# Stick-breaking half of the output projection begun between the pieces of the latent attention's preparation

## The chip, the cores and the metric

The kernel runs on one core of one Trainium2 chip. The metric is the device time of one execution in microseconds (us), given as the median of several runs. Names of engines in the profile: PE is TensorE's matmul queue, PEld its weight loads, DVE is VectorE, ACT ScalarE, POOL GpSimd, SP SyncE.

## The reference

Two transformer blocks act on 512 tokens of width 1024. The first is a hybrid of pooling and forgetting attention. The change lies in the second, which runs two attentions of 8 heads side by side, joins them, and then runs a feed-forward block over product keys. Cut to what matters:

```python
h = rms_norm(x, attn_norm)
sb_q, sb_k, sb_v, cq, ckv, k_pe = split(h @ w_in)
sb = stick_breaking_attention(sb_q, sb_k, sb_v)            # (512, 512)
q = rms_norm(cq, cq_norm) @ w_uq                           # 8 heads of 96
k_nope, v = split(rms_norm(ckv, ckv_norm) @ w_ukv)         # 8 heads of 64 + 64
k = concat(k_nope, k_pe)                                   # 8 heads of 96
q, k = rope_tail(rms_norm(q, q_norm)), rope_tail(rms_norm(k, k_norm))
mla = chunk_causal_softmax_attention(q, k, v)              # (512, 512)
mixed = concat(rms_norm(sb, sb_out_norm), rms_norm(mla, mla_out_norm))
x = x + mixed @ w_o                                        # (512, 1024) @ (1024, 1024)
x = x + peer_ffn(rms_norm(x, ffn_norm), ...)
```

The two norms before `w_o` are separate, so the half of the product that takes `sb` can be computed before `mla` is known.

## The kernel before

Tokens are kept in four tiles of 128 (`TT`). Weights come as a stream of units: a DMA on SP's queue into `wraw`, then a split into a high and a low part (`whi` by ACT, `wlo` by DVE or POOL, L129 and L130), each with two buffers. `unit(k, n)` takes the next unit of the stream and splits it if that hasn't been done; `ahead()` splits one unit more. Products use both parts: `mm3` issues three matmuls (L150 to L152) for each block of 128 rows.

In the second block two generators run against each other. The main one is `both`: first `sb_attention` (24 steps, three `yield`s in each, two or three heads' worth of scores, log, scan, exponential, transposes and values), then `ml_attention` (22 steps of scores, maximum, exponential, transposes, values). The other one, `fill`, holds everything that is done beside them: `heads_qk` (queries and keys of the stick-breaking heads), `prep` (the latent attention's preparation: cq and ckv with their norms, `uq_half`, `q_norm`, `uk_half`, `k_norm`, and `heads_T`, the transposes of the finished heads) and `after_prep`. For each `yield` of the main one, `fill` is advanced 0.65 steps during the stick-breaking attention (`RATE1`) and one step after it. Where the main one needs something of `fill` (scores of a query tile whose keys aren't there), it advances `fill` until it has come.

`after_prep` starts when `prep` is through and `sb_attention` has ended. It asks for the two rows of gains for the norms (`rows2`, in the buffer "ck", which `prep` uses for the latent keys), puts the norm of the stick-breaking half into the list `todo` (`o_norm`, three pieces for each token tile: `n0` sum of squares and reciprocal root, `n1` scaling, `n2` four transposes into the bank "mi" and the split into `mxs_hi` and `mxs_lo`), and takes one piece of `todo` at every second step. From its step 20 (`WP0`) on, every third step issues one tile of `wo_part`: two column halves of four token tiles each, 12 matmuls with 512 columns into "mi", which DVE adds to `xres`. The latent half's norms come into `todo` as its query tiles are done; its part of the projection comes after both attentions, with the final norm (`last2`).

A scheduler puts the instructions into the engines' queues. It goes by the order of the program as a priority and takes an instruction earlier where its inputs and buffers are there by its reckoning. Each engine then works through its own queue in order.

Of the kernel before, what the change touches and what calls it, by code (L numbers as in the profile page):

```python
# [11 lines left out]
F32R = mybir.dt.float32r  # L12
# [9 lines left out]
T = 512  # L22
TT = 4
# [14 lines left out]
ROWS = {}  # L38
# [22 lines left out]
def hybrid_mla_peer_kernel(ctx: ExitStack, tc: tile.TileContext, x, meta, gains, rows, bforget, wf, w1v, w1u, poolw,  # L61
                           wup, wout, pos, w2v, w2u, wcq, wckv, wuq, wukv, wo, wpq, skT, uT, peer_u, peer_v, out, stop=None):
    nc = tc.nc
    V, S, G, PE = nc.vector, nc.scalar, nc.gpsimd, nc.tensor
# [29 lines left out]
    def tB(shape, name, dt=F32, tag=None):  # L94
        return pB.tile(shape, dt, name=name, tag=tag, bufs=2 if tag == "sc" else 1)
# [18 lines left out]
    def load_next():  # L114
        i = st["load"]
        if i < len(stream):
            n = stream[i].shape[1]
            r = strm.tile([128, 2048], F32, name="wraw", tag="wraw")
            nc.sync.dma_start(r[:, :n], stream[i])
            raws[i] = (r, n)  # L120
            st["load"] += 1

    def split_next():
        i = st["split"]
        if i < len(stream):
            r, n = raws.pop(i)
            hi = strm.tile([128, 2048], F32R, name="whi", tag="whi")
            lo = strm.tile([128, 2048], F32R, name="wlo", tag="wlo")
            S.activation(hi[:, :n], r[:, :n], AF.Copy)  # L129
            lo_eng["e"].tensor_tensor(lo[:, :n], r[:, :n], hi[:, :n].bitcast(F32), op=OP.subtract)  # L130
            splits[i] = (hi, lo)
            st["split"] += 1

    def unit(k, n):
        i = st["use"]
        st["use"] += 1
        while st["split"] <= i:
            split_next()
            load_next()
        hi, lo = splits.pop(i)  # L140
        pat = "p (k n) -> p k n"
        return (hi[:, :k * n].rearrange(pat, k=k), lo[:, :k * n].rearrange(pat, k=k))

    def ahead():
        if st["split"] <= st["use"]:
            split_next()
            load_next()
# [10 lines left out]
    def row_of(dst, name, eng=None):  # L158
        o, w = ROWS[name]
        (eng or nc.scalar).dma_start(dst, rows[:, o:o + w].to_broadcast([dst.shape[0], w]))  # L160

    def rstd_from_ss(ss, n, p=128, cols=1):
        t = small.tile([128, 8], F32, name="rs_t", tag="rs_t")
        r = small.tile([128, 8], F32, name="rs_r", tag="rs_r")
        V.tensor_scalar(t[:p, :cols], ss, 1.0 / n, EPS, op0=OP.mult, op1=OP.add)
        G.tensor_tensor(r[:p, :cols], t[:p, :cols], mhalf[:p, :cols], op=OP.pow)
        return r[:p, :cols]
# [574 lines left out]
    with ExitStack() as c2:  # L742
        p2 = c2.enter_context(tc.tile_pool(name="p2", bufs=1))

        def t2(shape, name, dt=F32, tag=None, bufs=None):
            return p2.tile(shape, dt, name=name, tag=tag or name, bufs=bufs)
# [17 lines left out]
        row_of(mrow, "qk")  # L764
        crow = t2([128, 640], "crow")
        row_of(crow, "ckv")
        posf = t2([128, TT], "posf")
        V.tensor_copy(posf, posi)
        invf = t2([128, 16], "invf")
# [59 lines left out]
        sso, mv = so_[:, 0], so_[:, 1]  # L829
# [6 lines left out]
        def rope_ops(dst, src, tt, heads):  # L836

            c = cs[:, 0, tt, :].unsqueeze(1).to_broadcast([128, heads, 16])
            s = cs[:, 1, tt, :].unsqueeze(1).to_broadcast([128, heads, 16])
            ra = t2([128, 8, 16], "ra", bufs=2)[:, :heads]  # L840
            rb = t2([128, 8, 16], "rb", bufs=2)[:, :heads]
            a, b = src[:, :, 0:16], src[:, :, 16:32]
            G.tensor_tensor(ra, a, c, op=OP.mult)
            G.tensor_tensor(rb, b, s, op=OP.mult)
            ra2 = t2([128, 8, 16], "ra", bufs=2)[:, :heads]
            rb2 = t2([128, 8, 16], "rb", bufs=2)[:, :heads]
            G.tensor_tensor(ra2, a, s, op=OP.mult)
            G.tensor_tensor(rb2, b, c, op=OP.mult)
            G.tensor_tensor(dst[:, :, 0:16], ra, rb, op=OP.subtract)
            G.tensor_tensor(dst[:, :, 16:32], ra2, rb2, op=OP.add)  # L850

        def prep():
# [56 lines left out]
            def q_norm(tt):  # L909
                q = cn["qn", tt]  # L910
                ss8 = small.tile([128, 8], F32, name="ss8", tag="sum1")
                V.tensor_reduce(ss8, cn.pop(("ss", tt)), axis=AX.X, op=OP.add)
                r = rstd_from_ss(ss8, 96, cols=8)
                yield
                V.tensor_tensor(q, q, r.unsqueeze(2).to_broadcast([128, 8, 96]), op=OP.mult)
                rope_ops(q[:, :, 64:96], q[:, :, 64:96], tt, 8)
                yield
# [31 lines left out]
            def heads_T(which, tt, hg):  # L949
                if which not in mqk:  # L950
                    mqk[which] = tA([96, 8, T], "m" + which, tag="qk" if which == "qn" else "vz")
                src, dst = cn[which, tt], mqk[which]
                b = mm_bank()
                for hh in range(4):
                    PE.transpose(b[:96, tok(hh)], src[:, 4 * hg + hh, :], ident)
                bv = b[:96, :].rearrange("p (h t) -> p h t", h=4)
                (S.copy if hg else V.tensor_copy)(dst[:, 4 * hg:4 * hg + 4, tok(tt)], bv)
                yield
# [15 lines left out]
            for tt in range(1, TT):  # L974
# [9 lines left out]
                yield from nq  # L984
                yield from uq_half(us, tt, 1)
            u = unit(2, 1024)
            nq = q_norm(3)
            next(nq)
            yield from heads_T("qn", 1, 0)
# [13 lines left out]
            for tt in (1, 2, 3):  # L1003
                nk = k_norm(tt)
                next(nk)
                yield from heads_T("kn", tt - 1, 0)
                if tt < 3:
                    yield from uk_half(u, tt + 1, 0)
                yield from nk
                yield from heads_T("kn", tt - 1, 1)  # L1010
                mready.add(tt - 1)
                if tt < 3:
                    yield from uk_half(u, tt + 1, 1)
                if tt == 2:
                    ahead()
            yield from heads_T("kn", 3, 0)
            yield from heads_T("kn", 3, 1)
# [86 lines left out]
        todo = []  # L1104
        mixed = {}
        keep = {}
# [3 lines left out]
        def o_norm(src, key, half, tt):  # L1110
            def n0():
                keep[key] = col_of(p2, src, T)

            def n1():
                V.scalar_tensor_tensor(src, src, keep.pop(key), mixed["row"][:, half * 512:(half + 1) * 512],
                                       op0=OP.mult, op1=OP.mult)

            def n2():
                b = tr_tile(src, range(4), "mi", 1)
                dst = mixed[key[0]]  # L1120
                split_evac(dst[0][:, :, tok(tt)], dst[1][:, :, tok(tt)], b.rearrange("p (k t) -> p k t", k=4))

            return [n0, n1, n2]
# [56 lines left out]
        def wo_part():  # L1180

            for n in range(2):
                u = unit(4, 512)
                for tt in range(TT):
                    o = bank("mi", 1)
                    mm_group(o, lambda k: sel_of(mixed["s"], k, tok(tt)), u, 4)
                    if tt == 0:
                        ahead()
                    d = xres[:, tt, n * 512:(n + 1) * 512]
                    V.tensor_tensor(d, d, o, op=OP.add)  # L1190
                    yield

        def after_prep():

            rows2 = t2([128, 2, D], "rows2", tag="ck")
            mixed["row"], mixed["ffn"] = rows2[:, 0, :], rows2[:, 1, :]
            row_of(mixed["row"], "mix")
            row_of(mixed["ffn"], "ffn")
            mixed["s"] = (tB([128, 4, T], "mxs_hi", F32R, tag="sc"), tB([128, 4, T], "mxs_lo", F32R, tag="sc"))
            mixed["m"] = (tB([128, 4, T], "mxm_hi", F32R, tag="ut"), t2([128, 4, T], "mxm_lo", F32R, tag="cq"))  # L1200
            todo[0:0] = [f for qt in range(TT) for f in o_norm(sso[:, qt, :], ("s", qt), 0, qt)]
            wp = wo_part()
            cnt = 0
            while True:
                cnt += 1
                if todo and cnt % 2 == 0:
                    todo.pop(0)()
                if cnt >= WP0 and cnt % WPS == 0:
                    next(wp, None)
                if mixed.get("end"):  # L1210
                    for _ in wp:
                        pass
                    return
                yield

        def fill2():
            yield from heads_qk()
            yield from prep()
            while "sb_done" not in mixed:
                yield  # L1220
            yield from after_prep()

        def both(fill):
            yield from sb_attention(fill)
# [623 lines left out]
```

## Time and profile before

| | us |
|---|---|
| median of 3 runs | 2022.26 |
| lowest and highest | 2018.98, 2022.57 |
| the profiled execution | 2021.11 |
| its span in the trace | 2019.2 |
| TensorE busy in it | 1950.6 (97%) |
| DVE, ACT, POOL busy | 1372.6, 770.9, 582.2 |

Times in the rows below are microseconds from the start of the span. The stick-breaking attention ends at about 620, the latent attention at about 720, the projection and the final norm at about 760; the feed-forward block takes the rest. In the timeline a row gives the start, the duration, the engine, the line, the operation, output<-inputs, the count and, in brackets, how long the engine had stood idle before it and what released it. Ends of matmuls are modelled and overlap, so the time of one in a row of many is the distance of their starts.

### The profile page before, as it was taken

What the parts mean: (1) busy time and instruction counts of PE and PEld (TensorE: products, weight loads), DVE (VectorE), ACT (ScalarE), POOL (GpSimd) and SP (SyncE); (2) the same over time, 40 slices, a digit from 0 to 9 for tenths busy, and PEclk for the clock granted to TensorE, in tenths of its full rate; (3) what the DMA queues carried; (4) which work ended last, traced back from release to release, by engine and by line L of the source; (5) the groups of instructions that cost most, each with busy time, mean ns of one, the idle gap of its engine ahead of it and who ended that gap; (6) DMA issues with size and microseconds to landing.
All of it is one profiled execution on the core that took longest, in us unless ns stands there. A gap on an engine that the chain in (4) does not pass through costs nothing.

```text
span 2019.2 us, 26981 instructions
## 1 busy us (share of the span) xinstructions
PE 1950.6 (97%) x10297; PEld 1671.7 (83%) x10297; DVE 1372.6 (68%) x2571; ACT 770.9 (38%) x1228; POOL 582.2 (29%) x479
## 2 busy tenths in 40 slices
PE   7999999999998989999888999999999999999999
PEld 5777688877886779889888888888888888888887
DVE  4233423564476668999898677777777777787785
ACT  4223323254575442223555333333333333333332
POOL 1001100200147015655100143333333434343441
PEclk9999999999998999999999999999999999999999
DMA  4211122422111133213788888988888888888885
GB/s 150 97 63 42 42 84 88 142 92 73 36 54 63 42 136 105 94 43 105 225 251 243 288 305 320 317 310 312 286 316 286 315 318 314 307 321 296 308 297 191
DMA packets 138129, 387.63 MB, mean 192 GB/s; under 512 B 10624, under 2 KB 59904, under 8 KB 129808
## 3 DMA queue, kind: packets, MB, share of 16 engines
q1 hardware_dynamic: 48576, 216.65, 29.9%
q0 software_dynamic: 36864, 134.23, 19.5%
q10 hardware_dynamic: 52560, 35.03, 5.9%
q8 instruction: 80, 1.31, 0.3%
q14 instruction: 49, 0.40, 0.1%
HBM read 357.04 MB, written 28.84 MB: 191 GB/s over the span
## 4 chain that ended last, share of the span: by engine, by line
PE 73%; DMA 11%; DVE 7%; issue 4%; POOL 3%; ACT 2%; SPq 0%; DVEq 0%; POOLq 0%; ACTq 0%
PE mm L150 12%; PE mm L152 12%; PE mm L151 12%; DMA gat<-in_peer_v,idx 8%; PE s L151 3%; PE s L150 3%; PE s L152 3%; PE pt L151 3%; PE pt L152 3%; PE pt L150 3%; DMA gat<-in_peer_u,idx 2%; PE mi L150 1%; PE mi L152 1%; PE mi L151 1%; PE av L1044 1%
## 5 line engine op out<-in xcount | busy, mean ns | idle before, releaser
L1616 POOL DMA_INDIRECT gat<-in_peer_u,idx x128 | 172.0, 1344 | 413.0 <-DVE pre L1630 201.5
L1616 POOL DMA_INDIRECT gat<-in_peer_v,idx x128 | 166.4, 1300 | 265.0 <-DVE pre L1630 146.6
L1634 DVE SCALAR_TENSOR_TENSOR acc<-gat,pre,acc 128x1024 f32<-128x1024 f32 x128 | 164.1, 1282 | 77.1 <-DMA gat<-in_peer_v,idx 76.4
L152 PE MATMUL mm<-h_hi,ulo 128*128 128x384 f32 x568 | 192.2, 338 | 6.8 <-DVE ulo L1390 5.3
L1630 DVE CUSTOM_DVE_ANT_0 gat<-gat,xt 128x1024 f32<-128x1024 f32 x128 | 155.7, 1221 | 56.0 <-DMA gat<-in_peer_u,idx 55.5
L150 PE MATMUL mm<-h_hi,uhi 128*128 128x384 f32 x568 | 193.0, 340 | 0.0
L151 PE MATMUL mm<-h_lo,uhi 128*128 128x384 f32 x568 | 191.6, 337 | 0.0
L130 DVE TENSOR_TENSOR wlo<-wraw,whi 128x2048 fp32r<-128x2048 f32 (+1 forms) x42 | 96.0, 2285 | 136.4 <-ACT whi L129 136.3
L1389 ACT ACTIVATE vhi<-xt 128x1024 fp32r<-128x1024 f32 x94 | 99.5, 1059 | 215.2 <-PE mi L152 109.0
L152 PE MATMUL mm<-h_hi,h_lo 128*128 128x384 f32 x456 | 153.3, 336 | 4.5 <-POOL h_lo L1390 2.5
L150 PE MATMUL mm<-h_hi 128*128 128x384 f32 x456 | 153.9, 337 | 0.0
L151 PE MATMUL mm<-h_lo,h_hi 128*128 128x384 f32 x456 | 152.7, 335 | 0.0
L1390 DVE TENSOR_TENSOR vlo<-xt,vhi 128x1024 fp32r<-128x1024 f32 x94 | 114.7, 1221 | 53.6 <-ACT vhi L1389 53.4
L129 ACT ACTIVATE whi<-wraw 128x2048 fp32r<-128x2048 f32 (+2 forms) x53 | 97.5, 1840 | 110.7 <-PE mm L151 58.9
L152 PEld LDWEIGHTS mm<-h_hi,ulo 128*128 128x128 f32 x568 | 107.5, 189 | 8.7 <-DVE ulo L1390 6.9
L150 PEld LDWEIGHTS mm<-h_hi,uhi 128*128 128x128 f32 x568 | 107.6, 189 | 1.9
L151 PEld LDWEIGHTS mm<-h_lo,uhi 128*128 128x128 f32 x568 | 107.6, 189 | 1.9
L150 PE MATMUL mm<-hT_hi,whi 128*128 128x512 f32 x256 | 105.1, 410 | 1.3 <-DVE fz L417 1.0
L150 PE MATMUL s<-vhi,w_hi 128*128 128x512 f32 x256 | 100.3, 392 | 5.0 <-ACT w_hi L1710 5.0
L152 PE MATMUL mm<-hT_hi,wlo 128*128 128x512 f32 x256 | 102.2, 399 | 0.0
L151 PE MATMUL mm<-hT_lo,whi 128*128 128x512 f32 x256 | 102.1, 399 | 0.0
L151 PE MATMUL s<-vlo,w_hi 128*128 128x512 f32 x256 | 100.7, 393 | 0.0
(578 smaller groups left out, 5062.0 us busy)
## 6 DMA issues: line engine op xcount, KB each, us to landing
xt<-in_uT SPq DMA_DIRECT2D x98, 512.0 KB, 5.2
xt<-in_peer_v SPq DMA_DIRECT2D x94, 512.0 KB, 5.9
Gd<-stage ACTq DMA_DIRECT2D x24, 1024.0 KB, 5.3
gate<-Gd SPq DMA_DIRECT2D x16, 1536.0 KB, 10.0
raw<-in_peer_v SPq DMA_DIRECT2D x34, 512.0 KB, 5.4
wraw<-in_w1u SPq DMA_DIRECT2D x16, 1024.0 KB, 4.8
raw<-in_uT SPq DMA_DIRECT2D x30, 512.0 KB, 5.5
wraw<-in_wpq SPq DMA_DIRECT2D x8, 1024.0 KB, 4.8
```

The lines of the kernel that those rows point to most:

```text
L129: S.activation(hi[:, :n], r[:, :n], AF.Copy)
L130: lo_eng["e"].tensor_tensor(lo[:, :n], r[:, :n], hi[:, :n].bitcast(F32), op=OP.subtract)
L150: PE.matmul(o, L[0], R[0], start=start, stop=False)
L151: PE.matmul(o, L[0], R[1], start=False, stop=False)
L152: PE.matmul(o, L[1], R[0], start=False, stop=stop)
L1044: PE.matmul(av[:, col(h, qt):col(h, qt) + 64], pts[i][:, c + j * 128:c + (j + 1) * 128], src[:, j, h * 64:(h + 1) * 64], start=(j == 0), s ...
L1389: S.activation(hi, src, AF.Copy)
L1390: eng.tensor_tensor(lo, src, hi.bitcast(F32), op=OP.subtract)
L1616: G.indirect_dma_start(out=t, out_offset=None, in_=peer_u if kind == "u" else peer_v, in_offset=bass.IndirectOffsetOnAxis(ap=idx[:, s:s + ...
L1630: V.tensor_tensor_reduce(t, t, xt0, 1.0, 0.0, op0=OP.mult, op1=OP.add, accum_out=pre[:, s:s + 1])
L1634: V.scalar_tensor_tensor(acc, t, pre[:, s:s + 1], acc, op0=OP.mult, op1=OP.add)
```

## The change

- A tile `mrow0` of 128 x 512 is added; it gets the gains of the stick-breaking half's norm by a DMA on ACT's queue, at the start of the second block, and `n1` of that half reads it in place of `rows2`.
- `fill2` runs `prep` piece by piece. Once the stick-breaking attention has ended, each of its steps runs one piece of `after_prep` ahead of one piece of `prep`.
- `after_prep` first takes the 12 norm pieces of the stick-breaking half (in an order that staggers the token tiles) and then, when the unit of `w_ukv` has been taken from the stream, the four tiles of the first column half of `wo_part`. When `prep` is through it goes on as before with the rows, what is left of the norm pieces, and the second column half from step 20 on.
- Two `ahead()` calls get conditions, and one is added behind `prep`, so that the splits follow the new order of the units.

```diff
--- before.py
+++ after.py
@@ -764,6 +764,9 @@
         row_of(mrow, "qk")
         crow = t2([128, 640], "crow")
         row_of(crow, "ckv")
+        mrow0 = t2([128, 512], "mrow0")
+        o_ = ROWS["mix"][0]
+        nc.scalar.dma_start(mrow0, rows[:, o_:o_ + 512].to_broadcast([128, 512]))
         posf = t2([128, TT], "posf")
         V.tensor_copy(posf, posi)
         invf = t2([128, 16], "invf")
@@ -984,6 +987,7 @@
                 yield from nq
                 yield from uq_half(us, tt, 1)
             u = unit(2, 1024)
+            mixed["ukv"] = True
             nq = q_norm(3)
             next(nq)
             yield from heads_T("qn", 1, 0)
@@ -1011,7 +1015,7 @@
                 mready.add(tt - 1)
                 if tt < 3:
                     yield from uk_half(u, tt + 1, 1)
-                if tt == 2:
+                if tt == 2 and "wo" not in mixed:
                     ahead()
             yield from heads_T("kn", 3, 0)
             yield from heads_T("kn", 3, 1)
@@ -1112,7 +1116,7 @@
                 keep[key] = col_of(p2, src, T)
 
             def n1():
-                V.scalar_tensor_tensor(src, src, keep.pop(key), mixed["row"][:, half * 512:(half + 1) * 512],
+                V.scalar_tensor_tensor(src, src, keep.pop(key), mixed["row"][:, 512:1024] if half else mrow0,
                                        op0=OP.mult, op1=OP.mult)
 
             def n2():
@@ -1184,7 +1188,8 @@
                 for tt in range(TT):
                     o = bank("mi", 1)
                     mm_group(o, lambda k: sel_of(mixed["s"], k, tok(tt)), u, 4)
-                    if tt == 0:
+                    mixed["wo"] = mixed.get("wo", 0) + 1
+                    if tt == 0 and "prep_done" in mixed:
                         ahead()
                     d = xres[:, tt, n * 512:(n + 1) * 512]
                     V.tensor_tensor(d, d, o, op=OP.add)
@@ -1192,14 +1197,24 @@
 
         def after_prep():
 
+            mixed["s"] = (tB([128, 4, T], "mxs_hi", F32R, tag="sc"), tB([128, 4, T], "mxs_lo", F32R, tag="sc"))
+            parts = [o_norm(sso[:, qt, :], ("s", qt), 0, qt) for qt in range(TT)]
+            mine = [parts[i][k] for w in range(6) for i, k in ((w, 0), (w - 1, 1), (w - 2, 2)) if 0 <= i < TT]
+            wp = wo_part()
+            while "prep_done" not in mixed:
+                if mine:
+                    mine.pop(0)()
+                elif "ukv" in mixed and mixed.get("wo", 0) < TT:
+                    next(wp)
+                yield
             rows2 = t2([128, 2, D], "rows2", tag="ck")
             mixed["row"], mixed["ffn"] = rows2[:, 0, :], rows2[:, 1, :]
             row_of(mixed["row"], "mix")
             row_of(mixed["ffn"], "ffn")
-            mixed["s"] = (tB([128, 4, T], "mxs_hi", F32R, tag="sc"), tB([128, 4, T], "mxs_lo", F32R, tag="sc"))
             mixed["m"] = (tB([128, 4, T], "mxm_hi", F32R, tag="ut"), t2([128, 4, T], "mxm_lo", F32R, tag="cq"))
-            todo[0:0] = [f for qt in range(TT) for f in o_norm(sso[:, qt, :], ("s", qt), 0, qt)]
-            wp = wo_part()
+            todo[0:0] = mine
+            if mixed.get("wo", 0) > 0:
+                ahead()
             cnt = 0
             while True:
                 cnt += 1
@@ -1215,10 +1230,18 @@
 
         def fill2():
             yield from heads_qk()
-            yield from prep()
+            p, a = prep(), None
+            while "prep_done" not in mixed:
+                if next(p, p) is p:
+                    mixed["prep_done"] = True
+                    break
+                yield
+                if "sb_done" in mixed:
+                    a = a or after_prep()
+                    next(a)
             while "sb_done" not in mixed:
                 yield
-            yield from after_prep()
+            yield from a or after_prep()
 
         def both(fill):
             yield from sb_attention(fill)
```

## Rows read from the trace of the kernel before

**Rows 1.** The page, part 1: busy us, share, instructions by engine.

```profile
PE 1950.6 (97%) x10297; PEld 1671.7 (83%) x10297; DVE 1372.6 (68%) x2571; ACT 770.9 (38%) x1228; POOL 582.2 (29%) x479
```

**Rows 2.** Stretches: length, busy us by engine, granted clock, DMA share, GB/s.

```profile
620.00:630.00 10.00, 7.00 (x28) 5.39 (x29) 7.13 (x11) 5.24 (x15) 8.82 (x10) 0.83 0.53 197
630.00:640.00 10.00, 8.39 (x49) 6.37 (x48) 4.50 (x13) 3.42 (x10) 7.69 (x8) 1.00 0.03 11
...
650.00:660.00 10.00, 9.14 (x73) 7.89 (x72) 7.58 (x17) 7.16 (x20) 4.51 (x6) 1.00 0.14 53
660.00:710.00 50.00, 50.00 (x286) 38.88 (x285) 28.07 (x46) 19.53 (x48) 1.59 (x3) 1.00 0.12 43
```

**Rows 3.** Timeline of TensorE, gaps: start, us, instruction [idle <-releaser].

```profile
620.80 1.05 PE L955 MATMUL mm<-ident,qn 128*96 128x128 f32 x8 [0.81 <-ACT mqn L957]
622.56 0.78 PE L150 MATMUL mm<-whi,ck 128*128 128x512 f32 x1 [0.70 <-ACT mqn L957]
628.66 0.64 PE L955 MATMUL mm<-ident,qn 128*96 128x128 f32 x4 [1.50 <-POOL qn L850]
631.96 0.50 PE L150 MATMUL mm<-whi,ck 128*128 128x512 f32 x1 [0.83 <-ACT mqn L957]
634.85 0.50 PE L150 MATMUL mm<-whi,ck 128*128 128x512 f32 x1 [0.78 <-DVE mkn L957]
646.67 0.64 PE L955 MATMUL mm<-ident,qn 128*96 128x128 f32 x4 [0.62 <-POOL qn L945]
652.44 1.08 PE L955 MATMUL mm<-ident,qn 128*96 128x128 f32 x8 [0.85 <-POOL qn L945]
```

**Rows 4.** First norm's instructions (ns min/median/max, first, last start); DMA (KB, us to landing).

```profile
L171 ACT ACTIVATE junkb<-so x4: 629/630/632, 621.3 to 623.9; 128x512 bf16<-128x512 f32 x4
646.02 0.33 ACTq L160 DMA_DIRECT2D rows<-in_rows  x1
rows<-in_rows ACTq DMA_DIRECT2D x2, 512.0 KB, 3.5
652.35 2.23 POOL L166 TENSOR_TENSOR rs_r<-rs_t,mhalf 128x1 f32<-128x1 f32 x4
L1115 DVE SCALAR_TENSOR_TENSOR so<-so,rs_r,rows x4: 740/740/752, 652.9 to 666.3; 128x512 f32<-128x512 f32 x4
L156 DVE TENSOR_TENSOR mxs_lo<-mi,mxs_hi x4: 680/690/691, 659.6 to 673.7; 128x512 fp32r<-128x512 f32 x4
```

**Rows 5.** Tiles of the projection: their group, two timeline rows.

```profile
L150 PE MATMUL mi<-whi,mxs_hi x32: 392/399/800, 666.2 to 708.7; 128*128 128x512 f32 x32
675.76 0.39 PE L152 MATMUL mi<-whi,mxs_lo 128*128 128x512 f32 x1
677.86 0.40 PE L152 MATMUL mi<-whi,mxs_lo 128*128 128x512 f32 x1
```

**Rows 6.** Timeline of POOL and DVE, 620 to 651.

```profile
623.48 3.04 POOL L843 TENSOR_TENSOR ra<-qn,cs 128x128 f32<-128x128 f32 x1 [1.07 <-DVE qn L915]
623.92 2.28 DVE L130 TENSOR_TENSOR wlo<-wraw,whi 128x2048 fp32r<-128x2048 f32 x1
626.48 0.47 POOL L844 TENSOR_TENSOR rb<-qn,cs 128x128 f32<-128x128 f32 x1
630.45 1.65 POOL L166 TENSOR_TENSOR rs_r<-rs_t,mhalf 128x8 f32<-128x8 f32 x1 [0.46 <-DVE rs_t L165]
649.55 1.64 POOL L166 TENSOR_TENSOR rs_r<-rs_t,mhalf 128x8 f32<-128x8 f32 x1 [2.25 <-DVE rs_t L165]
```

**Rows 7.** Timeline of TensorE at the end of the latent attention.

```profile
711.38 1.00 PE L1044 MATMUL av<-so,pts 128*128 128x64 f32 x8
713.19 0.61 PE L1037 MATMUL pt<-ident,sbf 128*128 128x128 f32 x4
713.64 1.00 PE L1044 MATMUL av<-so,pts 128*128 128x64 f32 x8
```

## Prediction

> **What bounds the kernel now.** I read the page first [rows 1]: TensorE is busy 97% of the span, so a change of the order alone can only win time where TensorE stands idle or runs at its lower clock. Then the table of stretches around the place that the change touches [rows 2]: before 660 us TensorE idles (busy 7.00 of 10 us in 620 to 630, 8.39 in the next, 9.14 in 650 to 660); from 660 to 710 it shows no idle time at all. Its granted clock is 0.83 of full in 620 to 630, a part of that stretch being spent at 1.2 GHz and the rest at 2.4, and full after it. The timeline of TensorE names the gaps [rows 3]. Seven of them lie between 620 and 653: 0.81, 0.70, 1.50, 0.83, 0.78, 0.62 and 0.85 us, 6.09 us in all. All wait for a copy or a product of the latent attention's preparation (mqn, mkn, qn), by ACT, DVE or POOL. This is a chain of short steps in which TensorE has nothing else in its queue.
>
> What the change could put there runs later now. The norm of the stick-breaking half has its squares done by ACT from 621.3 on, as soon as the last heads are there, but its `pow` on POOL comes at 652.35 and its scaling on DVE at 652.9 [rows 4]. What holds it is the gain row: it lands in a buffer ("ck") that the preparation uses, so its DMA is issued at 646.02 and a transfer of this kind takes 3.5 us to land [rows 4]. The first tile of the projection starts at 666.2 [rows 5], in a stretch where TensorE is full anyway.
>
> **Where the pieces go.** The order written in the program is a priority; the trace shows instructions moved ahead of it wherever their inputs were there (the squares above). I count the `yield`s. `sb_attention` yields 3 x 27 = 81 times, at 0.65 that is 52 filler steps. `heads_qk` has 12, `prep` 64, so 24 pieces of `prep` are left when it ends, and the ukv unit is taken in step 50, before that. With the change each later step runs one piece of `after_prep` and one of `prep`: the 12 norm pieces in steps 53 to 64, the four tiles of the first column half in 65 to 68. Steps 53 to 66 are pulled before the latent attention's first scores (they wait for key tile 0, ready in step 66). So the norm and four of the eight stick-breaking tiles stand ahead of most of the latent attention. The other four stay behind `cnt` 20.
>
> **The change part by part.** Nothing is removed from TensorE. One tile is 12 matmuls; 9 of them take 677.86 - 675.76 = 2.10 us, 0.233 each [rows 5], so a tile is 2.80 us and four are 11.2. Four transposes take 713.64 - 713.19 = 0.45 us [rows 7], so the four norms 1.8. These 13.0 us leave the stretch after 653 and go to the one before it. If both stretches were full this would be worth 0; it is worth the idle time that they fill.
>
> When is the filler there? The first square ends at 621.9 (621.3 + 0.63), then come `pow` 0.56 (2.23 for four), scaling 0.74, transposes 0.45, ACT's copy (at about the 0.63 of the square) and DVE's difference 0.69 [rows 4, 7]: 3.1 us of bare work, so 625 at the earliest. The first two gaps (0.81 and 0.70, up to 622.56) are out of reach, and so is the half-clock stretch behind them (granted clock 0.83 in 620 to 630 [rows 2]). Within reach are the last five, 1.50 + 0.83 + 0.78 + 0.62 + 0.85 = 4.58 us. That is the upper bound of the plain gain.
>
> How much of it is filled? The transposes and the tiles share the one bank "mi": each norm holds it for 0.45 + 0.63 + 0.69 = 1.77 us, four for 7.1, and the first tile can follow at about 632 (625 + 7). So the gaps at 627.2, 631.1 and 634.1 meet mostly transposes of 0.45 us. I take 0.7, 0.6 and 0.6 of them, and all of the last two (0.62 and 0.85), which fall where a 2.8 us tile is waiting: **3.4 us**.
>
> Against it: four `pow` of 0.56 us on POOL, 2.2 us, now go into the stretch where POOL is busy 8.82 and 7.69 of 10 us [rows 2] and where TensorE waits for POOL's qn in three of the five gaps [rows 3]. POOL has holes (10 - 7.69 = 2.3 us idle in 630 to 640), and TensorE has a tile to do when one product is late; I charge a quarter, **0.5 us**; bounds 0 and 2.2. The split of the first wo unit (DVE 2.28 us at 623.92, [rows 6]) already lies there. The 256 KB DMA for `mrow0` is one more issue on ACT's queue behind those of mrow and crow, at the very start of this phase; an issue of this kind shows 0.33 us on the queue [rows 4], and the first use comes only after the last stick-breaking heads: 0, bounds 0 and 0.3. The DMA of rows2 stays behind `prep`, but only the latent half and the last norm read it now, later. The two moved `ahead()` calls concern the splits of the first and second wo unit; the trace shows the first one done at 626.2 [rows 6], long before its place in the program, so 0.
>
> What loses its cover? The later part of the latent attention has four tiles less beside it. Its bare step shows at the end [rows 7]: from one values product to the next, 711.38 to 713.64, 2.26 us, with scores, mask and transposes between them and no gap, and DVE and ACT are busy only 28.07 and 19.53 of the 50 us from 660 [rows 2]. So it is limited by TensorE without filler too: 0; if a step did wait 0.5 us, the eight steps of the last query tile would cost 4.
>
> Sum: -3.4 + 0.5 = -2.9 us. The profiled execution took 2021.11 us (2019.2 of it span), which gives 2018.2; the three runs have the median 2022.26 and lie between 2018.98 and 2022.57, and against the median I predict **2019.4 us**. The later phases shift as a block. A measurement of this kernel can tell about 0.2%, 4.0 us, from no change, so my forecast lies inside "same", near its edge.
>
> **A rule that speaks against it.** In the trace a POOL product of 128x128, 0.47 us the next time, took 3.04 us while DVE computed wlo for 2.28 us [rows 6]: 2.57 more, about the length of DVE's instruction. The Trainium skill, "SBUF — State Buffer", section "Who interferes with whom", says why: DVE and GpSimd share one pair of SBUF ports, as an exclusive lock for a whole instruction; by it DVE work with two SBUF inputs among POOL's products can cost POOL its full length. The trace agrees in kind. Here the four scalings (two SBUF inputs, 0.74 us each) move from 653, where POOL has little left, into POOL's chain; the rival below takes its price from these rows.
>
> **The rivals.**
> Full fill and a little more (faster). If the norms are through by 628, all 4.58 us go; if half of the clock loss of 620 to 630 (0.17 of 10 us, 1.7 us [rows 2]) comes back too, 5.4. With the two unreachable gaps it would be 6.1 + 1.7 = 7.8, which I exclude. It gives 2022.26 - 5 = 2017. For it: POOL stands idle for 1.07 us before 623.48 [rows 6], so the first norm's `pow` could slip in. Against it: the single "mi" bank.
> POOL as pacer (slower). TensorE takes its queue in order, so a tile that stands behind a transposition of qn cannot help it. The key chain has four rounds between 630 and 653 (POOL's `pow` of eight columns from 630.45 to 649.55, first and last in [rows 6]); each gets one more `pow`, 0.56, and one scaling that locks POOL, 0.74: 1.3 us a round, 5.2 in all, and nothing is won. It decides as soon as POOL's or DVE's extra work stands ahead of the chain's in their queues while TensorE's queue has the chain's transpose first. It gives 2022.26 + 5 = 2027. Against it: before these two `pow` POOL itself had waited 0.46 and 2.25 us for DVE, so it isn't the pacer in every round.
> Nothing moves. If the scaling waits all the same (for DVE, or behind the wo split on DVE), the norms come out around 640 and the tiles in a full stretch: -0.5 to 0 us, 2022.
> The latent attention runs dry (slower), +4 us as worked out above, 2026.
>
> **How the numbers follow.** Forecast case (1 to 4 us less) 0.45, full fill 0.32, nothing moves 0.09, POOL as pacer 0.10, running dry 0.04. So faster by over 0.2% 0.32, within 0.2% 0.54, slower 0.14. The range goes from the full fill with the clock, 2022.26 - 6.3 = 2016, down to 2015.5 for the spread of the runs, and up to 2024.5, which takes half of the pacer's price and leaves out its rest. The forecast case alone is 2018 to 2021.5.
>
> **What would show it.** Right: transposes of so between 625 and 636, mi tiles with mxs from about 630 to 650, TensorE's gaps after 626 down from 4.6 to 1 to 2 us, latent attention ending some 3 us earlier, still without gaps after 660. Wrong: `pow` of one column still late; rounds of the key chain longer than 6.4 us ((649.55 - 630.45) / 3) with TensorE idle in them; gaps between scores and transposes after 690; a lower clock after 630.

## The result and the profile after

| | before | after |
|---|---|---|
| median of 5 runs | 2022.26 us | 2034.6 us |
| lowest and highest | 2016.53, 2025.66 | 2026.48, 2038.61 |
| the profiled execution, its span | 2021.11, 2019.2 | 2026.48, 2024.8 |

The kernel before has two runs more here than in its table above. The changed kernel is slower: its time over that of the kernel before is 1.0056, 95% interval 1.0033 to 1.0079, so about 11 us. I had forecast 3 us less.

The profiled spans differ by only 5.6 us, and the feed-forward part, which nothing touched, varies by more than that: what follows the stage took 1265.3 and 1276.2 us in two executions of the changed kernel. So I measure the stage by itself, between two events that every kernel has: from the first product of the last query tile that waits for DVE's mqn, to the first low-part product of the feed-forward's queries. In the timeline of TensorE of the kernel before these are:

```profile
610.08 0.69 PE L150 MATMUL mm<-whi,cq 128*128 128x384 f32 x1 [1.65 <-DVE mqn L957]
...
749.62 0.58 PE L151 MATMUL s<-h_lo,whi 128*128 128x256 f32 x1 [4.11 <-DVE h_lo L156]
```

749.62 - 610.08 = 139.5 us. In the timeline of the changed kernel the same two events and all rows between 620 and 680 with an idle time (the bracket: how long TensorE stood, and for whom):

```profile
608.85 0.44 PE L150 MATMUL mm<-whi,cq 128*128 128x384 f32 x1 [1.65 <-DVE mqn L960]
...
620.41 0.79 PE L150 MATMUL mm<-whi,ck 128*128 128x512 f32 x1 [0.77 <-ACT mqn L960]
629.12 1.11 PE L197 MATMUL mi<-ident,so 128*128 128x128 f32 x4 [4.25 <-DVE so L1119]
634.92 0.50 PE L150 MATMUL mm<-whi,ck 128*128 128x512 f32 x1 [0.30 <-ACT mqn L960]
637.78 0.64 PE L958 MATMUL mm<-ident,qn 128*96 128x128 f32 x4 [1.19 <-POOL qn L948]
638.93 0.66 PE L197 MATMUL mi<-ident,so 128*128 128x128 f32 x4 [0.51 <-DVE mxs_lo L156]
640.31 0.61 PE L150 MATMUL mm<-whi,ck 128*128 128x512 f32 x1 [0.73 <-DVE so L935]
647.31 0.51 PE L150 MATMUL mi<-whi,mxs_hi 128*128 128x512 f32 x1 [0.84 <-DVE mxs_lo L156]
651.75 0.50 PE L150 MATMUL mi<-whi,mxs_hi 128*128 128x512 f32 x1 [0.35 <-DVE xres L1195]
670.87 0.70 PE L1145 MATMUL s<-mkn,mqn 96*128 96x256 f32 x2 [0.52 <-ACT sbf L1162]
673.70 1.08 PE L958 MATMUL mm<-ident,qn 128*96 128x128 f32 x8 [1.52 <-POOL qn L948]
...
759.54 0.58 PE L151 MATMUL s<-h_lo,whi 128*128 128x256 f32 x1 [4.11 <-DVE h_lo L156]
```

759.54 - 608.85 = 150.7 us: 11.2 us more, as much as the ratio says (how far single profiles of this stage differ is seen in experiment four). The five gaps from 626 to 653 that I wanted to fill [rows 3] summed to 4.58 us; from 621 to 653 there are now seven, 8.2 us in all, and two more behind 660, where TensorE had shown none. The largest, 4.25 us, stands before the first transposes of so, the norm's own piece. What those transposes waited for is seen in the timeline of DVE and POOL:

```profile
621.99 0.15 DVE L165 TENSOR_SCALAR rs_t<-ss 128x1 f32<-128x1 f32 x1
622.15 3.09 POOL L846 TENSOR_TENSOR ra<-qn,cs 128x128 f32<-128x128 f32 x1 [1.07 <-DVE rs_t L165]
622.65 2.28 DVE L130 TENSOR_TENSOR wlo<-wraw,whi 128x2048 fp32r<-128x2048 f32 x1
625.20 0.46 POOL L847 TENSOR_TENSOR rb<-qn,cs 128x128 f32<-128x128 f32 x1
627.27 0.56 POOL L166 TENSOR_TENSOR rs_r<-rs_t,mhalf 128x1 f32<-128x1 f32 x1
627.86 1.20 DVE L1119 SCALAR_TENSOR_TENSOR so<-so,rs_r,mrow 128x512 f32<-128x512 f32 x1 [2.87 <-POOL rs_r L166]
```

The first norm's small step on DVE was done at 622.1, as early as I had reckoned. Its `pow` then stood in POOL's queue behind the six rope products of the last query tile, and the first of these took 3.09 us in place of 0.46 beside DVE's 2.28 us split of the projection's first unit [rows 6 shows the same of before]. So `pow` began at 627.27, the scaling at 627.86, and TensorE, which works its queue in order, held the last query heads and the key pieces behind it back. Not all of the 4.25 us is new: TensorE stood at this place before too, for the query heads that the same six products finish (1.50 us [rows 3]).

The stretches of ten, columns as in [rows 2]:

```profile
620.00:630.00 10.00, 5.34 (x16) 4.08 (x17) 6.02 (x10) 3.76 (x11) 8.93 (x11) 0.67 0.42 153
630.00:640.00 10.00, 7.59 (x34) 5.48 (x32) 6.66 (x13) 3.27 (x8) 6.24 (x7) 0.81 0.00 1
640.00:650.00 10.00, 8.85 (x37) 7.01 (x37) 5.29 (x13) 2.72 (x7) 5.42 (x5) 0.83 0.00 0
650.00:660.00 10.00, 9.64 (x53) 7.48 (x52) 4.70 (x8) 3.02 (x16) 1.50 (x2) 1.00 0.01 2
660.00:710.00 50.00, 47.49 (x290) 37.17 (x288) 27.59 (x48) 23.26 (x57) 7.19 (x6) 1.00 0.18 64
```

TensorE's busy time from 620 to 630 fell from 7.00 to 5.34 us, and the granted clock is lower in three of these stretches where before only one was. One stretch earlier, still within the stage, it is the other way round: 1.00 in the changed kernel, and in the kernel before 0.71:

```profile
610.00:620.00 10.00, 9.92 (x54) 9.65 (x54) 7.03 (x10) 6.26 (x8) 9.15 (x12) 0.71 0.02 5
```

The changed kernel again, in steps of two:

```profile
626.00:628.00 2.00, 0.00 (x0) 0.00 (x0) 0.14 (x1) 0.00 (x0) 2.00 (x6) 0.72 0.76 266
628.00:630.00 2.00, 0.88 (x4) 0.88 (x5) 2.00 (x5) 0.00 (x0) 2.00 (x3) 0.50 0.56 234
630.00:632.00 2.00, 2.00 (x9) 1.76 (x8) 2.00 (x5) 0.60 (x1) 1.14 (x2) 0.50 0.00 0
632.00:634.00 2.00, 2.00 (x8) 1.47 (x8) 0.73 (x3) 0.26 (x1) 0.00 (x0) 0.57 0.00 0
```

TensorE did nothing from 626 to 628, and behind that it worked at 1.2 GHz up to 632 and somewhat longer. From 660 to 710 it is busy 47.49 of 50 us, where it had been busy all the time [rows 2].

### The profile page after: what moved, and what is told of

Its sections match the earlier page's. It is cut to its first block, busy times and chain, and to the rows that moved or that the text cites. A ratio compares the mean times of both kernels' runs of the same rounds, so it can differ in the third digit from the quotient of the medians.

```text
span 2024.8 us, 26977 instructions
## 1 busy us (share of the span) xinstructions
PE 1950.4 (96%) x10297; PEld 1669.5 (82%) x10297; DVE 1375.0 (68%) x2571; ACT 771.9 (38%) x1228; POOL 588.9 (29%) x479
## 3 DMA queue, kind: packets, MB, share of 16 engines
q0 software_dynamic: 36864, 134.23, 19.5%
## 4 chain that ended last, share of the span: by engine, by line
PE 77%; DVE 7%; DMA 6%; issue 3%; POOL 3%; ACT 2%; ACTq 0%; SPq 0%; DVEq 0%; POOLq 0%
PE mm L150 12%; PE mm L152 12%; PE mm L151 12%; DMA gat<-in_peer_v,idx 4%; PE s L151 4%; PE s L150 4%; PE s L152 4%; PE pt L152 4%; PE pt L151 4%; PE pt L150 4%; PE mi L150 1%; PE mi L152 1%; PE mi L151 1%; PE s L561 1%; PE av L151 1%
```

## The experiments

Two theories stood against each other. **A**: the norm's pieces stand in TensorE's queue ahead of preparation pieces that could have run, and wait for POOL. **B**: the four tiles stand ahead of the key chain and push the latent attention back.

**One: the norms without the tiles.**

```diff
-                elif "ukv" in mixed and mixed.get("wo", 0) < TT:
-                    next(wp)
```

> The changed kernel without the four tiles: only the twelve norm pieces stand among the pieces of the preparation, all eight tiles come behind the key chain as before. Theory A (TensorE's queue holds the norm's first transposes in front of the preparation's, and they wait for POOL's pow behind six rope products, 4.25 us in the changed kernel, then run on at 1.2 GHz): the wait stays at 4 to 4.5 us with the low clock behind it, and the time stays 6 to 11 us over the kernel before (+0.3 to +0.55%). Theory B (the tiles stand ahead of the key chain and push the latent attention back): the wait may stay, but the time falls to within 3 us of the kernel before.

Measured: 1.0040 (1.0017 to 1.0063), stage 146.0 us. The wait is there (timeline of TensorE):

```profile
630.49 1.11 PE L197 MATMUL mi<-ident,so 128*128 128x128 f32 x4 [3.31 <-DVE so L1119]
```

3.31 us, less than the 4 to 4.5 I expected, but there without any tile, so the norms alone cause it, and most of the loss stays. But the stage lost 4.7 us of its 11.2: both theories hold a part.

**Two: the root of the norms on ACT.**

```diff
-                keep[key] = col_of(p2, src, T)
...
+                S.activation(junkb[:, :T], src, AF.Square, accum_out=ss)
...
+                V.tensor_scalar(t[:, :1], ss, 1.0 / T, EPS, op0=OP.mult, op1=OP.add)
+                S.activation(r[:, :1], t[:, :1], AF.Ln)
+                S.activation(r[:, :1], r[:, :1], AF.Exp, scale=-0.5)
+                keep[key] = r[:, :1]
```

> The changed kernel with the reciprocal root of the four norms taken by ACT (logarithm, then exponential with factor -0.5) in place of POOL's pow; nothing else moves. Theory A: the scaling no longer waits for POOL's rope products, the first transposes wait under 1.5 us in place of 4.25, the low clock behind them goes or halves, and 6 to 9 us come back: the time is within 4 us of the kernel before. Theory B: it stays 8 to 11 us over the kernel before.

Measured: 1.0039 (1.0022 to 1.0057), stage 147.3 us. TensorE's queue has the same order:

```profile
625.75 0.66 PE L197 MATMUL mi<-ident,so 128*128 128x128 f32 x4 [0.85 <-DVE so L1129]
628.69 0.64 PE L958 MATMUL mm<-ident,qn 128*96 128x128 f32 x4 [2.29 <-POOL qn L853]
```

The wait of the first transposes falls from 4.25 to 0.85 us, as theory A said. But the query heads behind them now wait 2.29 us for POOL themselves, 3.14 us in the two places together, and less came back than it had said: 3.4 us of the stage, where I expected 6 to 9.

**Three: both edits together.** The two diffs above in one kernel.

> The changed kernel with both edits together: root of the four norms on ACT, and none of the four tiles among the preparation. If the costs of the norms' wait for POOL and of the tiles in front of the key chain add (3.4 us and about 4.6 us off the stage in the two single edits, of 11 that the change adds there), about 3 us remain: +0.1 to +0.2% over the kernel before. If each edit only removed the same loss, it stays at +0.35 to +0.4%.

Measured: 1.0000 (0.9979 to 1.0022), stage 143.6 us. In the stage the savings nearly add: 4.7 and 3.4 alone, 7.1 together. In the times the two edits took back 0.16 and 0.17% alone and 0.56% together; the intervals are too wide to tell whether that is more than the sum. What is left in the stage stands 0.7 us over another kernel in the order of before (142.9, next experiment) and 4.0 over the kernel before itself.

**Four: the row alone.** The kernel before with `mrow0` and the scaling that reads it, nothing else of the change.

```diff
+        mrow0 = t2([128, 512], "mrow0")
+        o_ = ROWS["mix"][0]
+        nc.scalar.dma_start(mrow0, rows[:, o_:o_ + 512].to_broadcast([128, 512]))
...
-                V.scalar_tensor_tensor(src, src, keep.pop(key), mixed["row"][:, half * 512:(half + 1) * 512],
+                V.scalar_tensor_tensor(src, src, keep.pop(key), mixed["row"][:, 512:1024] if half else mrow0,
```

> The kernel before with the row alone: its gains come early into mrow0 and the scaling reads them there; the order of the pieces is as before. My forecast held the norm back by the gain row's DMA. If that was right, pow and scaling of the stick-breaking half move from 652 to about 626 without any other edit. Theory A: the order of the program decides, so pow stays at about 650; the time is that of the kernel before within 0.2% and TensorE's gaps between 626 and 653 stay at 4 to 5 us in all.

Measured: 1.0001 (0.9980 to 1.0022), stage 142.9 us. The timeline of POOL has the four `pow` late all the same:

```profile
660.42 2.23 POOL L166 TENSOR_TENSOR rs_r<-rs_t,mhalf 128x1 f32<-128x1 f32 x4
```

So the row wasn't what held the norm in the kernel before. This kernel has the instructions of before in the order of before on TensorE, and its stage took 3.3 us longer in its profiled execution (one POOL wait of 2.92 in place of 1.50 us, the lower clock in another place): so far two profiles of one order can lie apart. Against this kernel the change adds 7.8 us to the stage, not 11.2. The wait and, of the stretches, the one with the lowest clock:

```profile
633.22 1.09 PE L958 MATMUL mm<-ident,qn 128*96 128x128 f32 x4 [2.92 <-POOL qn L853]
630.00:640.00 10.00, 6.41 (x20) 4.61 (x19) 4.07 (x9) 1.90 (x5) 7.99 (x11) 0.62 0.28 105
```

A granted clock of 0.62 from 630 to 640 is lower than in any stretch of ten of the changed kernel shown above, so the lower clock after 630 isn't a mark of the change.

This also tells what the 4.25 us are worth. How long TensorE stands there depends on how fast it did the products ahead, so the kernels go in pairs by their granted clock from 620 to 630. At 0.83 and 0.81, the kernel before waits 1.50 us and the norms without tiles 3.31; at 1.00, the row alone waits 2.92 and the changed kernel in its second execution (experiment eight) 4.67. In both pairs the order of the change adds 1.8 us, about the `pow` of 0.56 and the scaling of 1.20 that now stand ahead of the transposes.

**Five: the split in four.** DVE's low part of the projection's first unit in instructions of 512 columns.

```diff
-            lo_eng["e"].tensor_tensor(lo[:, :n], r[:, :n], hi[:, :n].bitcast(F32), op=OP.subtract)
+            for c in (range(0, n, 512) if i == 41 else (0,)):
+                sl = slice(c, c + 512) if i == 41 else slice(0, n)
+                lo_eng["e"].tensor_tensor(lo[:, sl], r[:, sl], hi[:, sl].bitcast(F32), op=OP.subtract)
```

> The changed kernel with the low part of the first projection unit computed by DVE in four instructions of 512 columns in place of one of 2048. If DVE's instruction holds POOL off for its whole length, the rope product that took 3.09 us beside it should take under 1.2 us, so that pow comes about 2 us earlier and the first wait falls from 4.25 to about 2; 2 to 4 us come back of the 11 that the change costs. If POOL is merely slow there, the product stays at about 3 us (or the six products together at about 5.1) and nothing comes back.

Measured: 1.0057 (1.0034 to 1.0081), stage 149.6 us. POOL's first rope product, a quarter of the split, POOL's second product, then TensorE's first wait:

```profile
623.78 0.92 POOL L848 TENSOR_TENSOR ra<-qn,cs 128x128 f32<-128x128 f32 x1 [1.07 <-DVE rs_t L167]
624.28 0.96 DVE L132 TENSOR_TENSOR wlo<-wraw,whi 128x512 fp32r<-128x512 f32 x1
624.66 0.91 POOL L849 TENSOR_TENSOR rb<-qn,cs 128x128 f32<-128x128 f32 x1
628.59 1.09 PE L199 MATMUL mi<-ident,so 128*128 128x128 f32 x4 [2.05 <-DVE rs_t L167]
```

The product takes 0.92 us beside a quarter of 0.96, in place of 3.09 beside the whole, and the next product 0.91. Alone each takes 0.46, so POOL loses 0.9 us to 0.96 us of DVE, where it lost 2.6 us to 2.28: the loss goes with the length of DVE's instruction. The Trainium skill, "SBUF — State Buffer", section "Who interferes with whom", says that a DVE instruction with two SBUF inputs contends with a GpSimd instruction that reads SBUF, over a port pair that is an exclusive lock. The two sums agree with that; that POOL is held to the end of DVE's instruction this run does not show, since its first product was done at 624.70 and the quarter at 625.24 (spans on POOL are rough). The wait was halved, to 2.05 us, but the time wasn't better: the quarters fell between other pieces, the query heads behind the transposes now waited 1.71 us for DVE, 3.76 us in the two places in place of 4.25, and the last key heads 2.00 us for POOL in place of 1.52.

**Six: a later start.** The pieces begin only when the last query heads are transposed; once with `pow`, once with the root on ACT.

```diff
+            mixed["q3"] = True
...
-                if "sb_done" in mixed:
+                if "sb_done" in mixed and "q3" in mixed:
```

> The changed kernel, but the pieces of the stick-breaking half start only when the last query heads are transposed, eight steps later; norms and four tiles then stand among the last key pieces. Theory A (the first transposes stand in TensorE's queue ahead of preparation pieces that were ready, and wait for POOL): the wait of 4.25 us and the low clock behind it are gone, and the time is that of the kernel before within 3 us, below it if the tiles fill the gaps of the last key rounds (2 to 3 us). Theory B (any filler ahead of the latent attention costs): still 5 to 8 us over the kernel before.

> The later start (behind the last query heads) together with the root of the four norms on ACT. The later start alone left +0.25%. If that rest is again the norms' pow and its neighbours on POOL, it goes to 0 within 0.15%. If it is the tiles themselves, which push the latent attention's exponentials and the split of the next unit together on DVE (there the values product waited 1.41 us for mlo, behind a split of 2.29 us), it stays at +0.15 to +0.3%.

Measured: 1.0025 (1.0005 to 1.0044) and 1.0049 (1.0025 to 1.0072), stages 147.7 and 149.0 us. The transposes of so no longer wait at that place, but the query heads do, 2.92 and 2.28 us for POOL, and the cost stays: 5 us with `pow`, the lower edge of theory B, and 10 us with ACT, more than either case that I had put down for it. With `pow`, the timelines of DVE and TensorE:

```profile
640.96 1.76 DVE L1120 SCALAR_TENSOR_TENSOR so<-so,rs_r,mrow 128x512 f32<-128x512 f32 x2
643.80 0.47 PE L150 MATMUL mm<-whi,ck 128*128 128x512 f32 x1 [0.93 <-DVE so L935]
681.69 2.31 PE L1049 MATMUL av<-so,pts 128*128 128x64 f32 x12 [1.41 <-DVE mlo L1180]
```

Two scalings stand on DVE ahead of the copy of the latent values that the next key tile's bank waits for (0.93 us there, 1.71 in the kernel with ACT), and later a values product waits 1.41 us for mlo, which stands behind the split of the next unit, 2.29 us on DVE. So theory A as I had put it, "the place in front of the query heads", is too narrow: wherever norms and tiles are put beside the key chain and the first latent steps, they meet an engine that the chain waits for.

**Seven: POOL out of the way.** The roots of the query and key heads' norms by ACT (`rstd_act`, the same two functions on 8 columns in place of `pow`): in the kernel before, whose four norms keep their late `pow`, and, together with the root of the four norms on ACT, in the changed one and in the changed one without the tiles.

```diff
...
-                r = rstd_from_ss(ss8, 96, cols=8)
+                r = rstd_act(ss8, 96, 8)
...
-                rb = rstd_from_ss(ss8, 96, cols=8).unsqueeze(2)
+                rb = rstd_act(ss8, 96, 8).unsqueeze(2)
```

> The kernel before, with the reciprocal roots of the query and key heads' norms taken by ACT (logarithm and exponential) in place of POOL's pow, which takes 1.65 us each for eight of them. If POOL paces the preparation, TensorE's gaps between 600 and 653 shrink by some 0.5 us at each of the four key rounds and at the queries' ones, and the time falls by 2 to 5 us (-0.1 to -0.25%). If DVE or the order in TensorE's queue paces it, nothing changes within 0.1%.

> The kernel before with the roots of the query and key heads' norms on ACT, a second time, for a narrower interval: 0.17% under the kernel before the first time, with an interval from 0.45% under to 0.12% over. If POOL paces the preparation, it is faster again, by 0.1 to 0.3%; if that was chance, the ratio comes out within 0.05% of one.

> The changed kernel with all these roots on ACT, those of the four norms and of the heads. If POOL is what the change collides with, its cost goes: within 0.1% of the kernel before with the same roots, or faster than it, since the tiles then fill the gaps. If the place in TensorE's queue is what costs (pieces in front of the key chain), it stays 0.2 to 0.4% over the kernel before.

> The changed kernel with all roots on ACT and without the four tiles among the preparation. Against the same kernel with the tiles (0.15% under the kernel before) it tells what the tiles are worth once POOL is out of the way: if they fill gaps, this one is 0.1 to 0.2% slower than that one; if they cost, it is 0.1 to 0.2% faster, so 0.25 to 0.35% under the kernel before.

| roots on ACT | ratio to the kernel before | 95% interval | stage, us |
|---|---|---|---|
| order of before (heads' roots) | 0.9983 | 0.9955 to 1.0012 | 137.6 |
| the same again | 0.9967 | 0.9945 to 0.9988 | 137.5 |
| the change (all roots) | 0.9985 | 0.9962 to 1.0008 | 139.8 |
| the change without the tiles (all roots) | 0.9989 | 0.9967 to 1.0012 | 137.8 |

The order of before with the heads' roots on ACT is faster than the kernel before (the second time clear of one, by about as much as expected) and than the changed kernel; the three versions with these roots on ACT can't be told apart by their times. With POOL relieved the change costs 139.8 - 137.5 = 2.3 us of the stage in place of 11.2: less than the two profiles of one order differed by in experiment four, and nothing that the times can tell. 2.0 of the 2.3 come with the tiles, 0.3 with the norms; the times show no gain from the tiles and no cost, where I had expected one or the other. So it is the meeting with the chain that runs through POOL that makes the change slow. The edit does two things at once, it takes `pow` off POOL and makes the chain's step shorter, and which of them counts isn't told apart here. Gaps of TensorE in the key rounds, first the order of before (with the heads' roots on ACT, second execution), then the change:

```profile
628.45 0.50 PE L150 MATMUL mm<-whi,ck 128*128 128x512 f32 x1 [0.77 <-DVE so L940]
631.48 0.50 PE L150 MATMUL mm<-whi,ck 128*128 128x512 f32 x1 [0.92 <-DVE so L940]
634.36 0.50 PE L150 MATMUL mm<-whi,ck 128*128 128x512 f32 x1 [0.78 <-DVE mkn L965]
```

```profile
628.24 0.50 PE L150 MATMUL mm<-whi,ck 128*128 128x512 f32 x1 [0.17 <-DVE so L943]
630.53 0.64 PE L966 MATMUL mm<-ident,qn 128*96 128x128 f32 x4 [0.62 <-DVE mqn L968]
635.03 0.50 PE L150 MATMUL mm<-whi,ck 128*128 128x512 f32 x1 [0.34 <-DVE so L943]
665.24 1.05 PE L966 MATMUL mm<-ident,qn 128*96 128x128 f32 x8 [0.44 <-DVE qn L955]
```

The tiles and norms do fill gaps here (0.77, 0.92 and 0.78 us become 0.17, 0.62 and 0.34), but as much stands elsewhere (0.44 before the last key heads, and several of 0.2): over the whole stage TensorE is idle for 10.6 us in both. So the 2.3 us don't stand in a wait; they are busy time, at a granted clock of 0.97 over the stage in both. Whether they are a cost at all, and what makes them, stays open.

**Eight: the changed kernel once more.**

> The changed kernel as it is, a second time, to see whether the wait is the same in another execution. If the order of the queues makes it, TensorE waits 3.5 to 4.5 us for the first scaled tile again, the stage from the fourth queries' product to the last normed tile takes 148 to 152 us in place of 139.5 to 143 for the two kernels in the order of before, and the time is 0.4 to 0.7% over the kernel before. If the first profile was an accident, stage and time come out within 0.2% of it.

Measured: 1.0056 (1.0033 to 1.0079), stage 765.13 - 613.10 = 152.0 us.

```profile
633.47 1.08 PE L197 MATMUL mi<-ident,so 128*128 128x128 f32 x4 [4.67 <-DVE so L1119]
```

4.67 us this time, a little above the 4.5 I had allowed, in the same place. The loss belongs to the order of the queues, not to one execution.

**The stage in two sums.** TensorE's time in the stage is busy time and idle time. The matmuls are the same in all these kernels, so busy time grows where they run at the lower clock or follow one another less closely. First the kernel before, then the changed one, over their stages, columns as in [rows 2]:

```profile
610.08:749.62 139.54, 128.22 (x736) 103.95 (x736) 88.77 (x145) 65.98 (x157) 44.35 (x48) 0.96 0.20 72
608.85:759.54 150.69, 131.64 (x737) 104.18 (x737) 90.41 (x145) 66.08 (x157) 47.49 (x48) 0.94 0.19 67
```

| kernel | stage | TensorE busy | idle |
|---|---|---|---|
| before | 139.5 | 128.2 | 11.3 |
| the row alone (order of before) | 142.9 | 129.6 | 13.3 |
| the change | 150.7 | 131.6 | 19.0 |
| the change again | 152.0 | 132.6 | 19.5 |
| norms without tiles | 146.0 | 132.4 | 13.7 |
| root of the norms on ACT | 147.3 | 129.7 | 17.6 |
| both edits | 143.6 | 128.6 | 15.0 |

The change adds 7.7 us of idle and 3.4 of busy time to the kernel before, 5.8 and 2.0 to the row alone. Without the tiles the idle time falls by 5.4 us, to that of the row alone, although the wait of 3.31 us stands there; with the root on ACT it falls by only 1.4, and the busy time is what comes back. So in these single profiles most of the added waiting hangs on the tiles, and the norms' `pow` costs less than the wait in front of its transposes suggests.

## Why the prediction was wrong

- **The step that failed: POOL's extra work charged at a quarter of 2.2 us.** I took POOL's idle time in the stretch as a store that four `pow` could draw on. What decided was the place in the queue: the first `pow` came behind six products that last 5.1 us together, and TensorE's next instruction hung on it. The row for this was there: the product of 3.04 us at 623.48 [rows 6], at the very time at which I let the first norm run. At that one place the order of the change adds 1.8 us to TensorE's wait (experiment four), against 0.5 us charged for all four norms.
- **Filling 3.4 of 4.58 us** didn't happen: in the stage TensorE's idle time grew by 7.7 us. The first tile began at 647.31, where I had said about 632, and the four stand ahead of the last key rounds, not in their gaps: the last key heads, at 652.44 before [rows 3], come at 673.70. A piece fills a gap only if it is ready when TensorE gets to it and the chain's next instruction isn't behind it. With POOL in the way there were five new waits by 652: four for the pieces' own inputs or bank (4.25, 0.51, 0.84, 0.35) and one of the key chain for a copy on DVE (0.73). With all roots on ACT the gaps did shrink, by 1.3 us in the three rows shown, without the idle time of the stage becoming less.
- **The tiles ahead of the key chain** were no term of the sum: I counted only what they fill and what cover they leave. Without them 5.4 us of the added idle time are gone (experiment one and the table behind experiment eight).
- **"Full clock after 630"** I carried over from the trace of before. Behind the wait of 4.25 us TensorE worked at 1.2 GHz again: granted clock 0.67, 0.81 and 0.83 from 620 to 650, where it had been 0.83 only in the first [rows 2]. My list of what would show the forecast wrong had it, the sum didn't. But the lower clock comes and goes with the execution (0.62 from 630 to 640 in the row alone), so it can carry only a part of the loss: over all executions of experiment eight the mean granted clock is 0.9842, against 0.9857 for the kernel before beside it. By my estimate that is 0.0015 of 2030, about 3 of the 11 us.
- **The gain row's DMA as what held the norm** was wrong (experiment four). The trace showed a DMA issued at 646 and a `pow` at 652, and I took the order of the two for a cause. It did not alter the sum, since the change moves the pieces anyway.
- **The split of the first wo unit at 0** was right as to its place, but it is the very instruction that stretched POOL's product by 2.6 us (experiment five), ahead of the moved `pow`.
- **Latent attention without the cover of four tiles at 0** held in the main: after 660 the changed kernel shows 0.52 and 1.52 us and two of 0.2. The 1.52 us is the wait for POOL's product of the last key heads, 0.85 us before [rows 3], which the tiles had pushed behind them. With a later start it cost more, 1.41 us for mlo.
- **The rival "POOL as pacer"** named the mechanism and the side (a tile behind a transposition can't help it; POOL's extra work ahead of the chain's). I gave it 0.10 and 5 us; the change cost 11, the clock and the tiles' own share with it. Nor did each key round get one of the four `pow`, as it says: three came from 627.27 to 631.14, ahead of the first key round's own at 634.88. What I set against it, that POOL had itself waited in some rounds, is true of the key rounds and says nothing of the first norm, which met POOL in the query round. The range ended at 2024.5 because it took in only half of that rival's price.

## What to carry to other kernels

Work that is to fill gaps on an engine that takes its queue in order must be ready without the engine that makes the gaps; otherwise it lengthens them, as four `pow` of 0.56 us did here, by 1.8 us at the first of them. Before counting gaps as room, follow the filler's own chain through every queue that it passes, and price it by what stands ahead of it there. Here the better lever was the slow step in the chain itself: a `pow` of 1.65 us on POOL against two ACT steps of 0.21 us each, 0.17 and 0.33% in two measurements, the second clear of no change, without any reordering.

## What the runs showed of the hardware

A POOL product can be held off by two DVE instructions in a row. In experiment two, timelines of POOL and DVE:

```profile
622.20 3.82 POOL L846 TENSOR_TENSOR ra<-qn,cs 128x128 f32<-128x128 f32 x1 [1.07 <-DVE rs_t L1123]
622.70 2.28 DVE L130 TENSOR_TENSOR wlo<-wraw,whi 128x2048 fp32r<-128x2048 f32 x1
624.96 0.74 DVE L1129 SCALAR_TENSOR_TENSOR so<-so,rs_r,mrow 128x512 f32<-128x512 f32 x1
```

The product of 0.46 us took 3.82 and was done 0.3 us after DVE's second instruction, though by the profile it had begun before the first (spans on POOL are rough). DVE suffers too: the scaling took 0.74 us in the kernel before [rows 4] and 1.20 us at 627.86 in the changed one, beside POOL's work.

The largest case of it I overlooked, because it is the same in every kernel here: TensorE's 4.11 us at the end of the stage (4.09 to 4.13 in the others). In the kernel before, POOL's split of the next unit and DVE's sum of one column:

```profile
743.94 4.83 POOL L130 TENSOR_TENSOR wlo<-wraw,whi 128x2048 fp32r<-128x2048 f32 x1 [1.00 <-ACT whi L129]
744.51 4.27 DVE L1257 TENSOR_TENSOR s2f<-ssf 128x1 f32<-128x1 f32 x1
```

The same sum took 0.15 us at 741.93. DVE's h_lo, for which TensorE waits, stands behind it. That is more than the change was meant to win; how much of it a split at another time would give back, no run here tried.
